# Results of the last three expert groups summed by one-hot matrices in PSUM, the row gathers of the others issued two groups earlier

## The chip, the core and the metric

The kernel runs on one core of one Trainium2 chip. The metric is the device time of one execution in microseconds (us). Engines: PE (matrix products), PEld (its weight loads), DVE (vector), ACT (scalar functions), POOL (general purpose, it also issues the indirect transfers on the software queue q0) and SP (issues the weight loads on the hardware queue q1). Tiles in SBUF have 128 partitions; products add up in eight PSUM banks of 128x512 f32, four called `pj` and four called `sc`.

## The reference

One block of a diffusion backbone over 512 latent tokens of width 1024 with 256 context tokens: two bidirectional recurrent mixers, then a mixture of 32 experts with two experts for a token, and a final norm. What concerns the change is the end:

```python
h_lat = h_lat + g1 * merge_branches(...)
h_lat = h_lat + g2 * hier_moe(modulate(rmsnorm(h_lat, norm_ffn), sh2, sc2), ...)
return rmsnorm(h_lat, norm_final)
# in hier_moe, for each expert e and the rows xb that go to it:
hid = silu(xb @ w_gate[e]) * (xb @ w_up[e])
y = hid @ w_down[e]
# each token gets the sum of its two rows y, each times its routing weight
```

## The kernel before

The experts' rows are packed into 18 groups of 128 slots, numbered 0 to 17 (`NG` is 18, `GROUPS` lists them): most groups hold two experts with 64 slots each, four hold one. Four experts are fixed to the first two groups, the others are put in by their count of tokens, the fullest first, so the last groups are the emptiest.

**The weights** of all experts are read once, 192 loads of 512 KB on SP (`feed`, L1122 and L1125), into a ring of 34 tiles called `raw` (`raw_tile`), in the order in which the products need them. A load waits for its tile to be free and for an earlier load to have landed.

**A group** g goes through `tokens` (its rows, gathered on POOL into `xg`, are transposed), `gate_up` (products L1156 into a `pj` bank, Silu on ACT, product on DVE: `hid`), `hidden` (transposes L1169, ACT copies `hT`, L1171) and `down` in two halves k of 16 products (L1180) into two `pj` banks. At the end of `down` DVE multiplies by the channel gate (`y`, L1189) and POOL scatters the rows to the table `ys_d` in DRAM, by token and choice (L1198). The loop interleaves: `gate_up(g)`, `down(g-1, 0)`, `hidden(g)`, `down(g-1, 1)`. For the last group (17) the rows are not scattered: `y` is multiplied by the slot's routing weight (L1194), split into two fp32r parts `yl` (ACT L1195, DVE L1196), and one-hot matrices `lsT` (made in `last_rows`, one 128x128 block for each of the four output tiles of 128 tokens) add them to the right tokens in PSUM (L1454).

**The end.** After `hidden(17)` `gather_results` issues eight gathers from `ys_d` (L986), two for each of the four output tiles i: one row for each choice of a token, 512 KB each, into free `raw` tiles `ya` and `yb`. The first waits for the scatter of group 16; a token whose expert is in the last group reads a row of zeros. `results` then sums: for tile 0 (`HD` is 1) DVE adds the weighted rows to the residual `hres` and then the PSUM banks; for tiles 1 to 3 PE first puts the residual into the bank by a product with the identity (L1452) and DVE adds the weighted rows to the bank (L1465, L1467). Then for each tile: ACT squares with a sum (L1468), a root (ACT L181, DVE L182 to L185), the product with the last norm's weights `nfin` and the root (tiles 0 and 1 on POOL L1471 and ACT L1472, tiles 2 and 3 on DVE L1474), and the output transfer on SP (L1475). An overflow block for experts with more rows than slots runs zero times with these inputs.

Instructions of an engine run in the order in which the scheduler put them. `issue_after(x)` keeps what it encloses behind instruction x in that order.

## Time and profile before

| | us |
|---|---|
| median of three runs | 1120.88 (1119.91 to 1122.23) |
| profiled execution | 1124.57 |
| its span in the profile | 1122.6 |
| PE busy | 1010.3 (90%) |
| DVE busy | 537.0 (48%) |
| ACT busy | 334.1 (30%) |
| POOL busy | 296.8 (26%) |

Times in the profile count from the start of the span. The experts' stage takes the time from some 850 us to the end. A share over the whole span says little about it; the stretches near the end and the DMA queues are to be read. DMA share is the mean busy share of the 16 DMA engines in a stretch.

### The profile page before, as it was taken

How to read it: one execution, taken by the hardware profiler on the slowest of the kernel's cores; microseconds unless marked ns; L12 is line 12 of the kernel's file. 1: busy time of each engine (PE TensorE's matmuls, PEld its weight loads, DVE VectorE, ACT ScalarE, POOL GpSimd, SP SyncE). 2: the span in 40 equal slices, each digit the busy share in tenths (PEclk: the TensorE clock that was granted, in tenths of full speed). 3: DMA queues.
4: the chain of work that ended last, by engine and by line, in shares of the span. 5: the costliest groups of instructions: out<-in, count | busy, mean ns of one | idle time of the engine just before them, and what ended most of it. 6: DMA issues, size and time to landing. Idle time of an engine off the chain costs nothing.

```text
span 1122.6 us, 17057 instructions
## 1 busy us (share of the span) xinstructions
PE 1010.3 (90%) x6574; PEld 825.9 (74%) x6574; DVE 537.0 (48%) x954; ACT 334.1 (30%) x580; POOL 296.8 (26%) x353
## 2 busy tenths in 40 slices
PE   3999899999899989999999999999837999999981
PEld 1679788799898978998977888889835665655430
DVE  4545677866788453554553341444461212212126
ACT  4237354554443213122323232332431101111003
POOL 1013235443536241415141100020431111110023
PEclk9999899999999999999999999999968999999996
DMA  9860213336224303341543161249159999999964
GB/s 303 210 207 20 57 38 95 94 95 207 57 76 114 95 19 94 111 134 38 151 136 108 40 177 65 86 158 379 53 194 385 409 405 399 393 391 401 403 260 181
DMA packets 111101, 203.19 MB, mean 181 GB/s; under 512 B 13147, under 2 KB 74925, under 8 KB 111018
## 3 DMA queue, kind: packets, MB, share of 16 engines
q1 hardware_dynamic: 98968, 180.53, 47.2%
q0 software_dynamic: 6320, 12.58, 3.1%
q10 hardware_dynamic: 5730, 8.98, 2.3%
q8 instruction: 52, 0.85, 0.3%
q14 instruction: 31, 0.25, 0.1%
HBM read 194.73 MB, written 17.31 MB: 189 GB/s over the span
## 4 chain that ended last, share of the span: by engine, by line
PE 29%; issue 19%; DVE 4%; POOL 3%; DMA 3%; ACT 0%; POOLq 0%; ACTq 0%; DVEq 0%
PE pj L341 16%; PE pj L332 9%; DMA raw<-ys_d,rowI 1%; POOL ys_d L1198 1%; POOL xg L986 1%; DMA xg<-xf_d,tokG 1%; DVE qs L594 1%; DVE oh L887 1%; PE sc L864 1%; DVE wl L1248 0%; PE sc L755 0%; PE sc L728 0%; DMA ys_d<-y,rowG 0%; DMA wada<-in_w_ada 0%; PE sc L555 0%
## 5 line engine op out<-in xcount | busy, mean ns | idle before, releaser
L332 PE MATMUL pj<-wh,xh 128*128 128x256 f32 x800 | 229.1, 286 | 3.6 <-ACT wh L1243 2.3
L332 PE MATMUL pj<-wl,xh 128*128 128x256 f32 x800 | 227.2, 285 | 0.3 <-DVE wl L1248 0.3
L332 PE MATMUL pj<-wh,xl 128*128 128x256 f32 x800 | 227.0, 284 | 0.0
L1248 DVE TENSOR_TENSOR wl<-raw,wh 128x1024 fp32r<-128x1024 f32 x88 | 118.5, 1354 | 93.0 <-ACT wh L1243 49.0
L332 PEld LDWEIGHTS pj<-wh,xh 128*128 128x128 f32 x800 | 153.8, 192 | 4.7 <-ACT wh L1243 2.5
L332 PEld LDWEIGHTS pj<-wh,xl 128*128 128x128 f32 x800 | 152.9, 191 | 0.6
L332 PEld LDWEIGHTS pj<-wl,xh 128*128 128x128 f32 x800 | 152.4, 191 | 0.7 <-DVE wl L1248 0.5
L1156 PE MATMUL pj<-raw,xt 128*64 128x256 f32 (+1 forms) x1024 | 135.0, 382 | 7.8 <-DMA raw<-in_w_expert_up 4.8
L1243 ACT CAST wh<-raw 128x1024 fp32r<-128x1024 f32 x88 | 91.4, 1048 | 168.7 <-PE pj L332 43.9
L1156 PEld LDWEIGHTS pj<-raw,xt 128*64 128x64 f32 (+1 forms) x1024 | 88.7, 143 | 53.4 <-DMA raw<-in_w_expert_up 8.1
L341 PE MATMUL pj<-xh,wh 128*128 128x512 f32 (+1 forms) x216 | 82.9, 388 | 3.3 <-ACT wh L1243 3.2
L341 PE MATMUL pj<-xl,wh 128*128 128x512 f32 (+1 forms) x216 | 82.8, 385 | 0.0
L341 PE MATMUL pj<-xh,wl 128*128 128x512 f32 (+1 forms) x216 | 82.5, 382 | 0.0
L341 PE MATMUL pj<-oT,wh 128*128 128x512 f32 x256 | 81.8, 399 | 0.8 <-ACT oT L760 0.5
L1180 PE MATMUL pj<-raw,hT 128*64 128x512 f32 (+1 forms) x256 | 75.8, 602 | 0.0
L703 DVE SCALAR_TENSOR_TENSOR adaacc<-wada,scT,adaacc 128x1024 f32<-128x1024 f32 x28 | 39.1, 1396 | 41.1 <-DMA wada<-in_w_ada 41.1
L341 PEld LDWEIGHTS pj<-oT,wh 128*128 128x128 f32 x256 | 48.3, 191 | 12.6 <-ACT oT L760 1.0
L341 PE MATMUL pj<-oT,wl 128*128 128x512 f32 x128 | 50.1, 394 | 0.0
L341 PEld LDWEIGHTS pj<-xh,wh 128*128 128x128 f32 x216 | 40.7, 190 | 11.0 <-ACT wh L1243 3.2
L1198 POOL DMA_INDIRECT ys_d<-y,rowG x17 | 16.9, 996 | 119.2 <-DVE y L1189 118.6
L423 POOL TENSOR_TENSOR th<-th,g 128x512 f32<-128x512 f32 x16 | 24.9, 1581 | 87.8 <-ACT th L422 87.8
L1189 DVE TENSOR_TENSOR y<-pj,adab 128x512 f32<-128x512 f32 x34 | 22.8, 689 | 51.5 <-PE pj L1180 51.5
(396 smaller groups left out, 1734.2 us busy)
## 6 DMA issues: line engine op xcount, KB each, us to landing
raw<-in_w_in SPq DMA_DIRECT2D x64, 512.0 KB
raw<-in_w_expert_up SPq DMA_DIRECT2D x64, 512.0 KB
raw<-in_w_expert_gate SPq DMA_DIRECT2D x64, 512.0 KB
raw<-in_w_expert_down SPq DMA_DIRECT2D x64, 512.0 KB
wada<-in_w_ada SPq DMA_DIRECT2D x32, 512.0 KB
wada<-in_w_ada SPq DMA_DIRECT2D x32, 256.0 KB
ys_d<-zero ACTq DMA_DIRECT2D x8, 512.0 KB
raw<-in_w_branch_gla SPq DMA_DIRECT2D x8, 512.0 KB
```

The costliest lines, as they stand in the source:

```text
L332: nc.tensor.matmul(out, x, (wh, wl)[wi][:, k], start=(start and first and k == 0 and n == 0), stop=(a == 1 and k == 3 and n == 2), skip_gr ...
L341: nc.tensor.matmul(out, (wh, wl)[wi][:, k, 128 * f:128 * (f + 1)], (th, tl)[xi][kk], start=(start and first and k == 0 and n == 0), stop=( ...
L423: nc.gpsimd.tensor_mul(th, th, g)
L594: nc.vector.tensor_mul(e, qT, qdec[:, None, o + 128 * h:o + 128 * (h + 1)].to_broadcast([128, 4, 128]))
L703: nc.vector.scalar_tensor_tensor(a, w, s, a, op0=OP.mult, op1=OP.add)
L864: nc.tensor.matmul(pl, hT[:, kk], wr[:, kk], start=(kk == 0), stop=(kk == NK - 1))
L1156: nc.tensor.matmul(p[r, u], st["x"][:, 4 * a + k, r], WT["gu", g, a, u, e][:, k], start=(a == 0 and u == 0 and k == 0), stop=(a == 1 and k ...
L1180: nc.tensor.matmul(st["p"][n2][r], st["h"][:, k, r], WT["d", g, k, 0, e][:, 512 * n2:512 * (n2 + 1)], start=(k == 0), stop=(k == 1))
L1189: nc.vector.tensor_mul(y[:, cs], st["p"][n2], ada_b[3][:, cs])
L1198: d = nc.gpsimd.indirect_dma_start(out=ys_d, out_offset=IOff(ap=rowG[:, g:g + 1], axis=0), in_=y, in_offset=None, bounds_check=ZROW - 1, o ...
L1243: nc.scalar.copy(parts[0], raw)
L1248: return nc.vector.tensor_sub(l, raws.pop(n), h)
```

## The change

`LAST` = 3 groups (15, 16, 17) now take the way that group 17 alone took: no scatter, but the slot's weight, a split into two fp32r parts (`tail`) and one-hot matrices (`LS["T"]`, three of them, made in `last_rows` in a loop over j). `gather_results` moves from behind `hidden(17)` to behind `gate_up(16)`: the gathers then wait for the scatter of group 14, and tokens of the last three groups read zeros. The new `early_sums` weights and adds the gathered rows to the residual ahead of the end: tiles 0 and 1 (`HD` = 2) on DVE, tiles 2 and 3 by scaled copies on ACT and adds on POOL. In `results` PE puts these sums into the banks of tiles 2 and 3 instead of the residual, and their squares and last norm read the banks directly. A root on ACT is issued before the end so that its table is loaded then.

```diff
-HD = 1
+HD = 2
+LAST = 3
...
 in down(g, k), after k == 1:
-            if g < NG - 1:
+        if g >= NG - LAST:
+            y = ring("y", g, 3, lambda: w4("y"))
+            h, l = (w4("tail", F32R) for _ in range(2))
+            tails.append((h, l))
+            w = LS["w"][:, g - NG + LAST:g - NG + LAST + 1]
+            for n2 in range(2):
+                cs = slice(512 * n2, 512 * (n2 + 1))
+                nc.vector.scalar_tensor_tensor(y[:, cs], st["p"][n2], w, ada_b[3][:, cs], op0=OP.mult, op1=OP.mult)
+                nc.scalar.copy(h[:, cs], y[:, cs])
+                last["part"] = nc.vector.tensor_sub(l[:, cs], y[:, cs], h[:, cs])
...
+    def early_sums(Y, r=range(4)):
+        for i in r:
+            ya, yb = Y[i]
+            if i >= HD:
+                for k, y in enumerate(Y[i]):
+                    nc.scalar.activation(y, y, AF.Copy, scale=wk[:, i, k:k + 1])
+                    nc.gpsimd.tensor_add(ya, y, hres[i] if k == 0 else ya)
+                continue
+            nc.vector.scalar_tensor_tensor(ya, ya, wk[:, i, 0:1], hres[i], op0=OP.mult, op1=OP.add)
+            nc.vector.scalar_tensor_tensor(ya, yb, wk[:, i, 1:2], ya, op0=OP.mult, op1=OP.add)
...
 in results(Y):
-                    nc.tensor.matmul(P[i, n], ident, hres[i][:, cs], start=True, stop=False)
+                    nc.tensor.matmul(P[i, n], ident, Y[i][0][:, cs], start=True, stop=False)
+            for j in range(LAST):
+                add(i, j)
...
+                s2 = small(1, "fs2")
+                for n, cs in enumerate(halves2):
+                    nc.scalar.activation(yb[:, cs], P[i, n], AF.Square, scale=1.0 / 32.0, accum_out=(s1, s2)[n])
...
 in the loop over g, after gate_up(g):
+            if g == NG - LAST + 1:
+                nfin = raw_tile(free)
+                nc.sync.dma_start(nfin, bass.AP(tensor=io["norm_final"].tensor, offset=io["norm_final"].offset,
+                                                ap=[[0, 128], [1, D]]))
+                Y = gather_results(lambda n: raw_tile(len(TL) + n))
...
         if g == NG - 1:
-            Y = gather_results(lambda n: raw_tile(free + 1 + n))
+            with tc.issue_after(last["hid"].ins), tc.issue_after(last["hT"].ins):
+                early_sums(Y, (0, 2, 3))
+            with tc.issue_after(last["part"].ins):
+                early_sums(Y, (1,))
+            with tc.issue_after(last["hT"].ins):
+                nc.scalar.activation(LS["r"], eps, AF.Sqrt)
```

**POOL, from the last gathers of tokens on.** `ys_d<-y` is a scatter, `raw<-ys_d` a gather of results. Before:

```order
L986 DMA xg<-xf_d,tokG 128x1024 x2
L1198 DMA ys_d<-y,rowG 1025x1024 x7
L986 DMA raw<-ys_d,rowI 128x1024 x8
L1471 TENSOR_TENSOR raw<-raw 128x1024 x2
L1075 TENSOR_LOAD extra
```

After:

```order
L987 DMA xg<-xf_d,tokG 128x1024 x2
L1203 DMA ys_d<-y,rowG 1025x1024 x5
L987 DMA raw<-ys_d,rowI 128x1024 x8
L1457 TENSOR_TENSOR raw<-raw,hres 128x1024
L1457 TENSOR_TENSOR raw<-raw 128x1024
L1457 TENSOR_TENSOR raw<-raw,hres 128x1024
L1457 TENSOR_TENSOR raw<-raw 128x1024
L1493 TENSOR_TENSOR raw<-raw 128x1024 x2
```

The gathers stand behind five scatters instead of seven, and four adds of the early sums stand between them and the products with `nfin`.

**ACT, from the last hT on** (the casts are the first fp32r parts of the last groups; `fs` are the sums of squares). Before:

```order
L1171 COPY hT<-sc 128x256
L1195 CAST yl<-y 128x512 x2
L1468 ACTIVATE raw,fs<-raw 128x1024
L181 ACT_TABLE_LOAD
L181 ACTIVATE fry<-fs,eps 128x1
```

After, with the tiles' numbers (`tail_9505` belongs to group 16, `tail_9536` to group 17):

```order
L1173 COPY hT_8014<-sc_9497 128x256
L1456 ACTIVATE raw_7782<-raw_7782,wk_191 128x1024
L1456 ACTIVATE raw_7784<-raw_7784,wk_191 128x1024
L1456 ACTIVATE raw_7786<-raw_7786,wk_191 128x1024
L1456 ACTIVATE raw_7788<-raw_7788,wk_191 128x1024
L1196 CAST tail_9505<-y_8047 128x512 x2
L1578 ACT_TABLE_LOAD
L1578 ACTIVATE wr_178<-eps_69 128x1
L1196 CAST tail_9536<-y_8201 128x512 x2
```

Four scaled copies of gathered rows (tiles 2 and 3) stand ahead of the casts of group 16, and the table load ahead of those of group 17.

**DVE, from the last hid on.** Before:

```order
L1162 TENSOR_TENSOR hid_7965<-hid_7965,pj_9369 128x256
L1189 TENSOR_TENSOR y_8047<-pj_9404,adab3_175 128x512
L1189 TENSOR_TENSOR y_8047<-pj_9405,adab3_175 128x512
L1194 SCALAR_TENSOR_TENSOR y_8201<-pj_9448,slotw_9241,adab3_175 128x512
L1194 SCALAR_TENSOR_TENSOR y_8201<-pj_9449,slotw_9241,adab3_175 128x512
L1196 TENSOR_TENSOR yl_9459<-y_8201,yl_9458 128x512
L1458 SCALAR_TENSOR_TENSOR raw_7786<-raw_7786,wk_191,hres_6774 128x1024
```

After:

```order
L1164 TENSOR_TENSOR hid_7965<-hid_7965,pj_9456 128x256
L1459 SCALAR_TENSOR_TENSOR raw_7665<-raw_7665,wk_191,hres_6774 128x1024
L1460 SCALAR_TENSOR_TENSOR raw_7665<-raw_7667,wk_191,raw_7665 128x1024
L1195 SCALAR_TENSOR_TENSOR y_8047<-pj_9491,wr_178,adab3_175 128x512
L1195 SCALAR_TENSOR_TENSOR y_8047<-pj_9492,wr_178,adab3_175 128x512
L1197 TENSOR_TENSOR tail_9506<-y_8047,tail_9505 128x512 x2
L1459 SCALAR_TENSOR_TENSOR raw_7768<-raw_7768,wk_191,hres_6776 128x1024
L1460 SCALAR_TENSOR_TENSOR raw_7768<-raw_7780,wk_191,raw_7768 128x1024
L1195 SCALAR_TENSOR_TENSOR y_8201<-pj_9526,wr_178,adab3_175 128x512
L1195 SCALAR_TENSOR_TENSOR y_8201<-pj_9527,wr_178,adab3_175 128x512
L1197 TENSOR_TENSOR tail_9537<-y_8201,tail_9536 128x512 x2
```

The sums of tile 0 come ahead of y of group 16, those of tile 1 ahead of y of group 17, and group 16 now has its two tail differences (L1197) there.

## Rows read from the trace of the kernel before

**Rows 1.** Busy time by stretch: columns named in the first row

```profile
core 0: us, PE busy (x) PEld busy (x) DVE busy (x) ACT busy (x) POOL busy (x), PEclk, DMA share, GB/s
1060.00:1070.00 10.00, 8.89 (x52) 4.14 (x50) 1.71 (x3) 0.76 (x2) 0.97 (x1) 1.00 1.02 404
1070.00:1080.00 10.00, 8.71 (x56) 4.10 (x52) 0.42 (x1) 0.38 (x1) 0.00 (x0) 1.00 1.01 397
1080.00:1085.00 5.00, 5.00 (x19) 2.20 (x18) 1.29 (x2) 0.37 (x1) 0.97 (x1) 1.00 0.27 111
400.00:404.00 4.00, 2.42 (x13) 1.51 (x11) 3.86 (x3) 0.00 (x0) 4.00 (x4) 1.00 0.00 0
404.00:408.00 4.00, 4.00 (x11) 3.20 (x12) 0.61 (x2) 0.00 (x0) 0.99 (x1) 0.57 0.00 0
```

**Rows 2.** Instructions in order of time, 1040 to 1124: start, us, engine, line [idle]

```profile
1051.86 0.97 POOL L1198 DMA_INDIRECT ys_d<-y,rowG  x1 [12.37 <-DVE y L1189]
...
1075.30 1.73 PE L1156 MATMUL pj<-raw,xt 128*64 128x256 f32 x13 [0.67 <-DMA raw<-in_w_expert_up]
...
1080.23 0.37 ACT L1171 COPY hT<-sc 128x256 f32<-128x256 f32 x1 [2.57 <-PE sc L1169]
...
1086.65 1.95 PE L1180 MATMUL pj<-raw,hT 128*64 128x512 f32 x8
...
1088.35 1.03 POOL L986 DMA_INDIRECT raw<-ys_d,rowI  x1 [3.73 <-issue]
1088.66 1.41 DVE L1194 SCALAR_TENSOR_TENSOR y<-pj,slotw,adab 128x512 f32<-128x512 f32 x2 [5.29 <-PE pj L1180]
...
1096.32 1.32 PE L1454 MATMUL pj<-yl,lsT 128*128 128x512 f32 x5
...
1109.80 1.06 ACT L1468 ACTIVATE raw<-raw 128x1024 f32<-128x1024 f32 x1
...
1112.52 1.28 DVE L1474 SCALAR_TENSOR_TENSOR raw<-raw,fry 128x1024 f32<-128x1024 f32 x1
```

**Rows 3.** DMA queues, 900 to 980: all, then the software queue

```profile
DMA packets 9852, 32.01 MB, mean 400 GB/s; under 512 B 2054, under 2 KB 2054, under 8 KB 9845
...
q0 software_dynamic: 2016, 3.41, 11.3%
```

**Rows 4.** The same, 980 to 1060; last row: scatters, us to landing

```profile
DMA packets 9518, 31.78 MB, mean 397 GB/s; under 512 B 1776, under 2 KB 1776, under 8 KB 9511
...
q0 software_dynamic: 1152, 1.24, 4.4%
...
ys_d<-y,rowG POOLq DMA_INDIRECT x6, 7.4
```

**Rows 5.** Chain of work that ended last: start, us, what

```profile
1083.64 3.65 DMA ys_d<-y,rowG
```

**Rows 6.** DMA queues, 1085 to 1123: packets, MB, share of 16 engines

```profile
q0 software_dynamic: 1296, 4.26, 31.9%
```

**Rows 7.** DMA queues of the page, whole span

```profile
q0 software_dynamic: 6320, 12.58, 3.1%
```

**Rows 8.** Groups by line, 1076 to 1123: busy us, mean ns, idle before

```profile
L1472 ACT ACTIVATE raw<-raw,fry 128x1024 f32<-128x1024 f32 x2 | 2.3, 1148 | 1.8 <-DVE fry L183 1.3 <-DVE fry L185 0.4
L1196 DVE TENSOR_TENSOR yl<-y,yl 128x512 fp32r<-128x512 f32 x2 | 1.4, 688 | 0.0
...
L1463 DVE TENSOR_TENSOR raw<-raw,sc 128x512 f32<-128x512 f32 x2 | 1.3, 680 | 0.0
```

**Rows 9.** Groups by line, POOL, whole span

```profile
L865 POOL TENSOR_TENSOR xf<-hres,adab 128x1024 f32<-128x1024 f32 x4 | 9.4, 2361 | 27.7 <-DVE hss L847 25.6 <-issue 2.2
```

**Rows 10.** Instructions in order of time, DVE beside POOL's product

```profile
1099.87 1.28 DVE L1467 SCALAR_TENSOR_TENSOR raw<-raw,wk 128x1024 f32<-128x1024 f32 x1
...
1100.44 6.21 POOL L1471 TENSOR_TENSOR raw<-raw 128x1024 f32<-128x1024 f32 x2 [1.55 <-ACT raw L1468]
...
1102.63 1.82 DVE L1467 SCALAR_TENSOR_TENSOR raw<-raw,wk 128x1024 f32<-128x1024 f32 x1
...
1104.37 2.30 DVE L184 SCALAR_TENSOR_TENSOR fra<-fry,frv 128x1 f32<-128x1 f32 x1
...
1107.51 0.21 DVE L184 SCALAR_TENSOR_TENSOR fra<-fry,frv 128x1 f32<-128x1 f32 x1
```

More of the change, by code (lines that the diff above doesn't have):

```diff
@@ L1161, in gate_up @@
         nc.scalar.activation(hid, p[:, 0], AF.Silu)
-        nc.vector.tensor_mul(hid, hid, p[:, 1])
+        last["hid"] = nc.vector.tensor_mul(hid, hid, p[:, 1])
         st["hid"] = hid
@@ L1170, in hidden @@
         h = m1k("hT", g).rearrange("p (k t) -> p k t", t=128)
-        nc.scalar.copy(h, p)
+        last["hT"] = nc.scalar.copy(h, p)
         st["h"] = h
@@ L1440, in gather_results, with add @@
         return y
+    def early_sums(Y, r=range(4)):
[8 more added lines that the diff above has]
+            nc.vector.scalar_tensor_tensor(ya, yb, wk[:, i, 1:2], ya, op0=OP.mult, op1=OP.add)
     def results(Y):
         P = {}
+        halves2 = [slice(512 * n, 512 * (n + 1)) for n in range(2)]
+        def add(i, j):
+            for n, cs in enumerate(halves2):
+                for m, x in enumerate(tails[j]):
+                    nc.tensor.matmul(P[i, n], LS["T"][j][:, i], x[:, cs], start=(i < HD and j == m == 0),
+                                     stop=(j == LAST - 1 and m == 1))
         for i in range(4):
[L1447 to L1449 removed]
+            for n, cs in enumerate(halves2):
                 P[i, n] = sc() if i < 2 else pj()
                 if i >= HD:
[L1452 to L1454 removed]
+                    nc.tensor.matmul(P[i, n], ident, Y[i][0][:, cs], start=True, stop=False)
+            for j in range(LAST):
+                add(i, j)
         for i, (ya, yb) in enumerate(Y):
@@ L1471, in results @@
                 nc.gpsimd.tensor_mul(yb, ya, nfin)
-                nc.scalar.activation(ya, yb, AF.Copy, scale=rs)
+                nc.scalar.activation(yb, yb, AF.Copy, scale=rs)
             else:
-                nc.vector.scalar_tensor_tensor(ya, ya, rs, nfin, op0=OP.mult, op1=OP.mult)
-            nc.sync.dma_start(io["out"][0, 128 * i:128 * (i + 1)], ya)
+                for n, cs in enumerate(halves2):
+                    nc.vector.scalar_tensor_tensor(yb[:, cs], P[i, n] if i >= HD else ya[:, cs], rs, nfin[:, cs],
+                                                   op0=OP.mult, op1=OP.mult)
+            nc.sync.dma_start(io["out"][0, 128 * i:128 * (i + 1)], yb)
     ada = late_ada()
```

84 lines of the change are left out of this document (35 added, 49 removed).

## The prediction

> **What bounds the kernel now.** I read three views in this order: the busy time by stretch near the end, the DMA queues of the same stage, and the instructions in order of time from the last products on.
>
> The stretches [rows 1] show that until 1080 us the 16 DMA engines are the limit: their share is 1.01 to 1.02 at 397 to 404 GB/s, while PE is busy 8.7 to 8.9 of 10 us. PE catches up with the stream: the last gate/up products start only when their weights land, after 0.67 us of waiting [rows 2]. After 1080 the stream is over (share 0.27). Two stretches of 80 us earlier in the same stage carry 3.41 and 1.24 MB on the software queue q0, and the total is 400 and 397 GB/s [rows 3, 4]: what the gathers and scatters move is taken from the weights, it does not come on top.
>
> From there the end is a chain [rows 2]. H, the copy of hT of the last group, ends at 1080.60. The last down product ends at 1088.60, 8.0 us after H. The last scatter lands 3.65 us after 1083.64 [rows 5], so the eight gathers start only at 1088.35. The last output tile is normed by 1113.80, which is H + 33.2, and 8.8 us of output transfer and program end follow to the span's 1122.6. The profiled execution took 1124.57 us, the median of the three runs is 1120.88; I work out a difference against the span and add it to the median.
>
> **The change part by part.**
>
> *The gathers move ahead of the weights' end.* They now wait for the scatter of group 14, issued at 1051.86 [rows 2], which lands some 7.4 us later in the full stream [rows 4], so at about 1060 instead of 1088. POOL issues nothing for the experts after that, so nobody on POOL queues behind them. But their bytes fall into the stretch where the DMA engines have no room. In the kernel before, q0 moved 4.26 MB after 1085 and kept all engines busy for 31.9% of 38 us, 12.1 us [rows 6]; at the 401 GB/s of the stage 4.26 MB are 10.6 us. Bounds: 0, if the engines found room, to 12.1. I take 10.6, the nearer stage. Against that one of the two dropped scatters (groups 15 and 16) lay in the stream: all gathers and scatters of tokens are 12.58 - 4.26 = 8.3 MB [rows 6, 7], in 35 transfers, so 0.24 MB or 0.6 us for one; these groups are the small ones, I take 0.3. Whether the weights of the last gate/up feel all of it depends on how the engines share. A scatter of the stage lands after 7.4 us [rows 4] against 3.65 in quiet [rows 5], so it is not put behind everything that is queued, and I take half and half: the 4.26 MB are through by 1060 + 21 = 1081, before the last gate/up weights, and H moves by **+10.3 us**.
>
> The rows cannot show the arbitration itself. The Trainium skill ("DMA: Bandwidth & Descriptors", Queues, rings and completion order) states that an engine goes round its queues packet by packet, which is the half and half of the sum; with the weights first the sum would be the second rival's. The same page (Specifications) gives a fabric ceiling of 435 GB/s; if the mix could reach it, 34 GB/s for 21 us would hide 0.7 MB and the term would be an estimated 1.8 us smaller, but the stage shows 400 at a share above 1, so the row stands.
>
> *One-hot matrices for three groups instead of one* (last_rows): 16 more small products, 8 more transposes and as many DVE comparisons, written among the products of group 15, some 30 us before H. PE has 1.1 to 1.3 us of slack in 10 [rows 1] and gets 10 more by the term above, so they cost nothing; without that cover they would cost a few us once.
>
> *From H to the last output.* ACT now runs four scaled copies of the gathered rows right after hT, 1.15 us each [rows 8], to H + 4.7, ahead of the casts of group 16; POOL adds each to the residual, four times 2.36 us [rows 9], from H + 1.2 on. DVE meanwhile has the two tail differences of group 16 (0.69 each [rows 8]), the sums of tile 1 (two of 1.28) and then the last y (1.41 [rows 2]). What happens when POOL and DVE both read two SBUF operands is in [rows 10]: a 1.28 us sum beside POOL's product takes 1.82, and a 128x1 step of 0.21 takes 2.30 and ends at 1106.67, when POOL's second product ends (1106.65); the two waited for each other in turn, one instruction each, and POOL's took 3.1 instead of 2.36. The first rows stretch the sum only a little, the last rows fully; I take the full alternation, since the tiny step lost all of the product's time. Then: adds 1 and 2 end at H + 5.9; the first difference ends at 6.6, add 3 at 9.0, the second difference at 9.7, add 4 at 12.0, DVE's tile-1 sums at 14.6, y at 16.0, its cast and differences at 17.4. PE's last down product stands behind the products of group 16, which need the second difference: 9.7 + 0.9 + 1.95 = 12.5, hidden under y's wait. The products of group 17 then run: 4 for the first two tiles, 12 for tile 2, two of the residual and 12 for tile 3, at 0.26 us each [rows 2] and about 0.5 for the fp32 two, so tile 2 is summed at 20.8 and tile 3 at 24.5. On ACT the order is square 0, root, square 1, scale 0, root, squares of tile 2, scale 1, root, squares of tile 3: DVE's adds (0.68 each [rows 8]) give tile 0 at 19.0, square 20.2, POOL's product 22.6, scale 0 at 24.1, tile 2's halves 26.1, scale 1 at 27.2, tile 3's halves from 27.5. The last tile needed 4.0 us from its square to the end before (1109.80 to 1113.80 [rows 2]); with a split square it is 4.7, so the last norm ends at H + 32.2. Before it was H + 33.2: **-1.0 us**. Without the alternation the same chain ends at H + 26.9, **-6.3 us**; these are the two ends. The early table load and the second tile with HD = 2 are inside these chains.
>
> The Trainium skill ("SBUF — State Buffer", Who interferes with whom) calls the port that DVE and GpSimd share an exclusive lock, held for a whole instruction by a GpSimd operation that reads SBUF and a DVE one with two SBUF inputs. By it the term is the -1.0; no row shows that such a step could run through a POOL add.
>
> Sum: +10.3 - 1.0 = +9.3 us, 1120.88 + 9.3 = **1130.2**.
>
> **The rivals.**
>
> 1. *No alternation* (the DVE steps fall between the adds): +10.3 - 6.3 = +4.0, 1124.9. For it: 0.7 us steps fit gaps while ACT feeds POOL. Against: ACT is ahead of POOL, so POOL has no gaps, and the 2.30 us step [rows 10].
> 2. *Weights first*: the gathers get little until the weights are in. H moves little, but rows 4 to 7 of Y then land near 1092 to 1094, ACT waits for them in front of the casts of group 16, PE's last down products and y stand behind; last norm some 6 us later than before, 1124.7 to 1126.7. This is also the case that the change does not do what it says: the sums run behind the products, not beside.
> 3. *Room in the DMA engines*, the other side: gathers move at 1060 to 1081 without delaying a weight, the delay is 0, and the tail gives 1.0 to 6.3 us: 1114.6 to 1119.9. Faster is decided where the delay is under 4 us with no alternation. Against: share 1.02 and the nearly equal totals of [rows 3, 4]; for: the one with more on q0 is 3 GB/s the higher.
> 4. *PE's clock*: at half rate of the weights PE waits some 3 us between bursts of 2 us. After a stretch with 2.42 busy of 4 us the granted clock was 0.57 in the next one (1.2 GHz would be 0.50) [rows 1]. If it is low at the last two down products (1.95 us each), up to 3.9 us more: 1134.
>
> **How the numbers follow.** Forecast 0.50 at 1130.2; rival 1 0.17; rival 2 0.13; rival 3 0.11; rival 4 0.09. Within 0.2% means 2.2 us, about what a measurement tells from no change, so 1118.6 to 1123.1. Faster: most of rival 3 and a shorter chain than worked out, 0.11. Same: the rest of rival 3 and the low end of rivals 1 and 2, 0.10. Slower: 0.79. Range: low 1121 leaves out rival 3; high is the 12.1 us bound with part of rival 4, 1120.88 + 12.1 - 1.3 + 3 = 1135.
>
> **What would show it.** In the trace after: gathers issued near 1060; q0 and q1 sharing about 400 GB/s from 1060 to 1081; PE waiting 2 to 4 us for gate and up weights in the last two groups instead of 0.6; the weights' end near 1091 and the copy of hT near 1091. If that copy still ends near 1081 to 1083 while the gathers have landed, the main term is wrong. For the tail: POOL adds of 3 us or more and a DVE difference or tile-1 sum of over 2 us; last norm 30 to 33 us after hT. If all DVE steps keep 0.7 and 1.3 us, rival 1 holds.

## The result and the profile after

The changed kernel takes 1137.75 us (median of four runs, 1133.25 to 1139.2) against 1120.54 us for the kernel before (four runs, 1119.91 to 1122.23): a ratio of 1.0144 with an interval of 1.0114 to 1.0175. Slower was right; the time lies above the range of the prediction (1121 to 1135). In a second comparison on another chip it was 1138.81 against 1128.14, a ratio of 1.0098 (1.0059 to 1.0136). The profiled execution took 1133.25 us, its span is 1131.4.

**Where to count from.** Raw times of two profiles can't be laid side by side: the stage ahead of the last groups ends several microseconds earlier or later in each execution, of one and the same kernel too. I count from W, the moment at which SP issues the first gate weights of the last group. This is the row of before, in order of time on SP (start, us, engine, line):

```profile
1055.09 1.62 SPq L1122 DMA_DIRECT2D raw<-in_w_expert_gate  x2
```

and of after, with the last expert weights that SP issues, eight loads of down weights (the columns are the same):

```profile
1050.98 1.62 SPq L1124 DMA_DIRECT2D raw<-in_w_expert_gate  x2
...
1061.23 9.84 SPq L1127 DMA_DIRECT2D raw<-in_w_expert_down  x8
```

W was 1055.09 and 1059.14 in two executions of before, 1050.98, 1056.64 and 1055.42 in three of after. From W to the end of the span the two of before need 67.5 and 69.0 us (mean 68.2), the three of after 80.4, 80.1 and 82.1 (mean 80.9). By this the change costs **12.6 us**; the forecast was 9.3. The timed differences, 17.2 and 10.7, lie around it. On the median of before 12.6 us would be 1133.1, inside the range; the 4.6 us beyond it lie ahead of W (in the second comparison this part is -1.9), and no run shows what sets W. So that the time lies above the range is owed to that part, and that 12.6 is near 9.3 is in part luck, since its parts are others:

| us after W | before | after |
|---|---|---|
| scatter of group 14 issued | -3.2 | +10.9 |
| first gather of results issued | +33.3 | +19.4 |
| H, end of the last copy of hT | +25.5 | +29.7 |
| y of group 17 begins | +33.6 | +53.0 |
| last norm ends | +58.7 | +71.7 |
| span ends | +67.5 | +80.4 |

H comes 4.1 us later, and from H to the last norm it takes 42.1 us instead of 33.2, 8.9 more. The forecast had 10.3 and -1.0.

**Why H is late.** Busy time of the engines in three stretches of after (columns as in [rows 1]), the middle one being that in which the products for the one-hot matrices are strung through those of group 15:

```profile
1030.00:1037.00 7.00, 5.93 (x37) 3.58 (x36) 4.81 (x20) 0.00 (x0) 1.03 (x1) 1.00 1.02 403
1037.00:1051.00 14.00, 13.83 (x57) 7.78 (x58) 3.71 (x16) 0.58 (x1) 0.00 (x0) 0.53 1.02 401
1051.00:1060.00 9.00, 9.00 (x57) 4.54 (x59) 1.02 (x2) 1.34 (x3) 0.00 (x0) 0.98 1.03 411
```

The granted clock falls to 0.53 for 14 us (0.50 is the lower level, 1.2 GHz) while PE is busy 13.83 of 14. PE's own rows (start, us, line, what, how many):

```profile
1028.24 0.95 PE L1227 MATMUL sc<-wk,lsh 128*128 128x1 f32 x8
...
1041.80 1.87 PE L1227 MATMUL sc<-wk,lsh 128*128 128x1 f32 x8
1043.60 1.12 PE L1158 MATMUL pj<-raw,xt 128*64 128x256 f32 x4
```

Eight of the small products (128x1 out) took 0.95 us at full clock and 1.87 here, and four gate/up products took 1.12 us (0.65 in e9 below, at full clock). The ACT row of `hid` that needs the products of group 15 begins at +5.3 by W (1056.30) instead of -10.2 (1044.85), 15.5 us late; the scatter of group 14 is issued at +10.9 instead of -3.2, 14.1 us late; `hid` of groups 16 and 17 is 9.9 and 4.9 us late, and H 4.1.

**Where the rows are.** POOL, in order of time: the scatter of group 14, the first of the eight gathers, the first and the last of the four adds:

```profile
1061.86 0.97 POOL L1203 DMA_INDIRECT ys_d<-y,rowG  x1 [26.97 <-DVE y L1202]
1070.38 1.03 POOL L987 DMA_INDIRECT raw<-ys_d,rowI  x1 [7.55 <-DMA raw<-in_w_expert_down]
...
1089.06 2.34 POOL L1457 TENSOR_TENSOR raw<-raw,hres 128x1024 f32<-128x1024 f32 x1 [8.09 <-ACT raw L1456]
...
1096.22 2.68 POOL L1457 TENSOR_TENSOR raw<-raw 128x1024 f32<-128x1024 f32 x1
```

The gathers stand 14 us later by W than the forecast put them (1060 less 1055.09, so +5), when nearly all gate/up weights are in. So they take next to nothing from those; the share of the DMA engines stays at 1.03 up to 1085, and the rows of tiles 2 and 3, which ACT scales, land after H (those of tile 0 are there at 1078.84, when DVE sums them). ACT, in order of time: copy of hT, the scaled copies of the rows, the casts of group 16 and those of group 17:

```profile
1080.26 0.37 ACT L1173 COPY hT<-sc 128x256 f32<-128x256 f32 x1 [1.80 <-PE sc L1171]
1087.83 1.15 ACT L1456 ACTIVATE raw<-raw,wk 128x1024 f32<-128x1024 f32 x1 [7.20 <-DMA raw<-ys_d,rowI]
1089.72 3.65 ACT L1456 ACTIVATE raw<-raw,wk 128x1024 f32<-128x1024 f32 x3 [0.74 <-DMA raw<-ys_d,rowI]
1093.28 1.12 ACT L1196 CAST tail<-y 128x512 fp32r<-128x512 f32 x2
...
1104.85 1.24 ACT L1196 CAST tail<-y 128x512 fp32r<-128x512 f32 x2 [8.94 <-issue]
```

Behind the copy of hT ACT has nothing before the scaled copies. It waits 7.2 us for the first row of tile 2 and then for the second, and the casts of group 16, whose y has been ready since 1085, stand behind them until 1093.28. What hangs on the casts, on DVE:

```profile
1093.91 5.53 DVE L1197 TENSOR_TENSOR tail<-y,tail 128x512 fp32r<-128x512 f32 x2 [9.00 <-ACT tail L1196]
...
1104.02 1.41 DVE L1195 SCALAR_TENSOR_TENSOR y<-pj,wr,adab 128x512 f32<-128x512 f32 x2 [2.06 <-PE pj L1182]
...
1121.29 1.41 DVE L1497 SCALAR_TENSOR_TENSOR raw<-pj,fry,raw 128x512 f32<-128x512 f32 x2
```

and on PE:

```profile
1093.93 0.79 PE L1470 MATMUL sc<-tail,lsT 128*128 128x512 f32 x1 [7.97 <-ACT tail L1196]
...
1101.50 2.44 PE L1182 MATMUL pj<-raw,hT 128*64 128x512 f32 x8
```

PE waited 7.97 us for the casts. Two differences that take 1.31 us alone (the row of group 17 at 1105.50) took 5.53 beside POOL's adds. PE's last down product, behind the products with these parts, ran at 1101.50 and y followed at 1104.02; the answering row of before is that of y in [rows 2], 1088.66. The last norm began at 1121.29 and ended at 1122.70. The stretches of after behind the stream (the last two rows have the lower clock):

```profile
1080.00:1085.00 5.00, 5.00 (x24) 2.17 (x24) 2.81 (x4) 0.37 (x1) 0.98 (x1) 1.00 1.03 413
1085.00:1090.00 5.00, 0.97 (x6) 0.08 (x2) 0.00 (x0) 1.43 (x2) 0.94 (x1) 0.89 0.47 190
1090.00:1095.00 5.00, 0.79 (x1) 0.29 (x1) 1.09 (x1) 4.77 (x6) 4.92 (x3) 0.50 0.02 9
1095.00:1100.00 5.00, 1.72 (x3) 1.00 (x4) 5.00 (x3) 0.91 (x2) 3.82 (x2) 0.50 0.00 0
```

The first of them is W + 29 to 34, and the same stretch of before (1084.1 to 1089.1) has a DMA share of 0.07 instead of 1.03. Then PE is busy for 3.5 of 15 us.

### The profile page after: what moved, and what is told of

Its sections match the earlier page's. It is cut to its first block, busy times and chain, and to the rows that moved or that the text cites. A ratio compares the mean times of both kernels' runs of the same rounds, so it can differ in the third digit from the quotient of the medians.

```text
span 1131.4 us, 17244 instructions
## 1 busy us (share of the span) xinstructions
PE 1024.5 (91%) x6642; PEld 837.3 (74%) x6642; DVE 546.6 (48%) x988; ACT 342.0 (30%) x595; POOL 303.4 (27%) x355
## 5 line engine op out<-in xcount | busy, mean ns | idle before, releaser
L1158 PE MATMUL pj<-raw,xt 128*64 128x256 f32 (+1 forms) x1024 | 138.2, 391 | 2.1 <-DMA raw<-in_w_expert_up 2.1
L1182 PE MATMUL pj<-raw,hT 128*64 128x512 f32 (+1 forms) x256 | 71.6, 606 | 0.0
L704 DVE SCALAR_TENSOR_TENSOR adaacc<-wada,scT,adaacc 128x1024 f32<-128x1024 f32 x28 | 39.5, 1409 | 42.3 <-DMA wada<-in_w_ada 42.3
L342 PEld LDWEIGHTS pj<-xh,wh 128*128 128x128 f32 x216 | 40.9, 190 | 10.9 <-ACT wh L1251 3.2
L342 PEld LDWEIGHTS pj<-xl,wh 128*128 128x128 f32 x216 | 41.1, 190 | 8.1 <-DVE xl L316 0.4
L342 PEld LDWEIGHTS pj<-xh,wl 128*128 128x128 f32 x216 | 41.1, 190 | 7.9 <-DVE wl L1256 0.5
## 6 DMA issues: line engine op xcount, KB each, us to landing
raw<-in_w_expert_up SPq DMA_DIRECT2D x64, 512.0 KB, 10.7
```

What stands on the lines that cost most here:

```text
L342: nc.tensor.matmul(out, (wh, wl)[wi][:, k, 128 * f:128 * (f + 1)], (th, tl)[xi][kk], start=(start and first and k == 0 and n == 0), stop=( ...
L704: nc.vector.scalar_tensor_tensor(a, w, s, a, op0=OP.mult, op1=OP.add)
L1158: nc.tensor.matmul(p[r, u], st["x"][:, 4 * a + k, r], WT["gu", g, a, u, e][:, k], start=(a == 0 and u == 0 and k == 0), stop=(a == 1 and k ...
L1182: nc.tensor.matmul(st["p"][n2][r], st["h"][:, k, r], WT["d", g, k, 0, e][:, 512 * n2:512 * (n2 + 1)], start=(k == 0), stop=(k == 1))
```

## The experiments

The theory after the first profile: (a) the early gathers do share the stream half and half, but in after they come too late to fall on H; (b) they come late because the one-hot work slows PE; (c) the rows then stop ACT in front of the casts. The main rival was the prediction's own sum: the stream term alone, whatever PE does. All times below are from W; ratios are against the kernel before on the same chip.

**The change again**, untouched, profiled once (e1), then profiled and timed (e5):

> The changed kernel once more, for a second trace. Clock theory: the 24 small products and 12 transposes of the one-hot matrices, written among group 15's products, bring the granted clock to 0.50 (in the first trace from 1037 to 1051 us), PE falls some 11 us behind, the scatter of group 14 and with it the gathers come some 10 us later than the weights allow, and the rows land at 1089. Then this trace shows 0.50 there again, and a run that is 4 to 6 us longer than the first has either a longer stretch at 0.50 or a second one nearer to the end. Stream theory (the forecast): the copy of hT of the last group is late because the gathers hold back the last gate and up weights; then PE waits on weights in the last two groups. 1133 to 1139 us by both.

> The changed kernel timed on this chip. Counted from W, the issue of the last group's first gate weights, the kernel before ends at W + 67.5 us and the changed one at W + 80.4 and W + 80.1 (two traces), so the change itself is worth 12.7 us; what the first comparison showed beyond that (17.2) would be where W fell by chance. Then the ratio here is 1.0113, some 12 to 13 us. If the change also moves W, it is 1.0144 again, 16 us or more.

Measured: 1138.45 us in the first, with the scatter of group 14 at +12.2, H at +34.4 and the end at +80.1; in the second the ratio 1.0098 told above, the scatter at +10.9, H at +29.7, the end at +82.1. The late scatter and the late end are there each time. The interval of 1.0098 holds the 1.0113 that was expected if W fell late by chance, and not the 1.0144 of the other reading. In the first, H was 4.7 us later than in the others, by a stop of ACT (last section), and the end was not: H does not set it, the copies of the rows do (they end at +42.4, +42.4 and +42.3 in the three).

**One matrix made, copied for the two other groups** (e2):

```diff
-        for j in range(LAST):
+        for j in (LAST - 1,):
...
+        for j in range(LAST - 1):
+            nc.scalar.copy(LS["T"][j], LS["T"][LAST - 1])
+            nc.vector.tensor_copy(LS["w"][:, j:j + 1], LS["w"][:, LAST - 1:LAST])
```

> Only group 17's one-hot matrix is worked out, as in the kernel before; those of groups 15 and 16 are copies of it, so 16 small products and 8 transposes are left out (the output then lacks the right rows of these two groups), and all else is as in the changed kernel. Clock theory: the granted clock stays 1.00 from 1020 to 1060 us, the scatter of group 14 is issued near 1048, the gathers near 1056, they now meet the last gate and up weights, so the copy of hT moves some 10 us (as the forecast had it) and the tail behind it takes 32 us instead of 42: 1130 us, and 1126 if the tail has no alternation. If the small products are not the cause: 1137 as the changed kernel.

Measured: ratio 1.0068 (1.0046 to 1.0090), end at +77.2. The output lacks the right rows of groups 15 and 16; the work on them behind their matrices is the same. The scatter is issued at -3.2 as before, the first gather at +4.6, and the clock is 1.00 from 1020 to 1070, in the stretch with the small products too:

```profile
1030.00:1040.00 10.00, 8.96 (x52) 4.68 (x53) 2.73 (x9) 0.76 (x2) 0.00 (x0) 1.00 1.01 402
```

Now the stream term falls where the prediction put it: PE waits for the last up weights.

```profile
1088.92 1.73 PE L1158 MATMUL pj<-raw,xt 128*64 128x256 f32 x13 [1.36 <-DMA raw<-in_w_expert_up]
```

DMA queues from 1068 to 1075 (packets, MB, share of 16 engines):

```profile
q1 hardware_dynamic: 381, 1.41, 51.9%
q0 software_dynamic: 365, 1.34, 49.2%
```

and SP's last eight loads:

```profile
1071.22 18.10 SPq L1127 DMA_DIRECT2D raw<-in_w_expert_down  x8
```

Each queue has half of the engines, with nearly as many packets as the other (381 and 365); issuing eight loads takes SP 18.10 us, where they took 9.84 in after. H is at +35.7, so it moved by 10.2 us, and from H to the last norm it takes 32.8; the prediction said 10.3 and 32.2. The steps between agree too: POOL's second and fourth add end 5.9 and 11.5 us after H (5.9 and 12.0 in the prediction), DVE's sums of tile 1 at 13.9 (14.6), y at 15.5 (16.0). Packet by packet is what the Trainium skill ("DMA: Bandwidth & Descriptors", Queues, rings and completion order) states; these rows agree.

**The one-hot work earlier**, at `g == 9`, so among the products of group 10 (e3):

```diff
-        if g == NG - 4:
+        if g == 9:
```

> All three one-hot matrices are worked out five groups earlier, among group 10's products instead of group 15's; nothing else moves. Clock theory: the stretch at 0.50 moves with them to some 80 to 90 us earlier, PE is level with the weights again before group 15, the rest as with one matrix: 1130 us. If the work itself costs PE the time wherever it stands, or the loss is in the tail alone: 1137.

Measured: 1.0073 (1.0044 to 1.0102), end at +79.8: the expectation fails. The stretches of this kernel (columns as above):

```profile
960.00:1000.00 40.00, 38.83 (x200) 23.04 (x198) 13.31 (x46) 2.39 (x6) 4.05 (x4) 0.74 1.03 405
...
1020.00:1060.00 40.00, 39.92 (x292) 22.86 (x290) 8.30 (x14) 4.03 (x9) 3.92 (x4) 1.00 1.01 397
```

The low clock came along (0.74 in the mean of 40 us), and PE did not catch up: it is busy 39.92 of 40 us from 1020 on, at full clock. By W, `hid` of group 10 is 20.5 us late and the scatter of group 14, at +9.0, still 12.2: in these groups there is little slack to catch up in, since PE of before is busy 94.61 of the 100 us from 960 to 1060.

**Is it the count of small products, or the four slots?** The kernel before writes its comparisons into eight slots, the change into four (`m % 4`), so that DVE must wait for PE before it writes the next four. First the kernel before with its one-hot work done three times (e9; `again` overwrites the same result):

```diff
+        for again in range(3):
+            pw = sc((128, 1))
...
```

> The kernel before, with its one group's one-hot matrix worked out three times over in the same place, so that only PE's 16 added small products and 8 added transposes and DVE's comparisons are new; gathers, sums and order are those of before. Small-products theory: group 15's products take some 14 us longer on PE (in the changed kernel the scatter of group 14 stood at W + 10.9 instead of W - 3.2, W being the issue of the last group's first gate weights), part of it is made good while PE has weights in stock, the copy of hT of the last group comes at W + 29 to 30 instead of W + 25.5, and the end at W + 70 to 72 instead of W + 67.5: 3 to 5 us slower than before. My own prediction's step (these products cost nothing): W + 67.5, no change.

Measured: 0.9984 (0.9959 to 1.0010), end at +68.3 (before 67.5 and 69.0). Its stretch with the small products:

```profile
1029.00:1043.00 14.00, 14.00 (x100) 9.65 (x100) 8.02 (x32) 2.13 (x4) 0.98 (x1) 1.00 1.01 395
```

The clock stays at 1.00, and H is at +25.6 (25.5 in before). But the scatter of group 14 is at +1.4 instead of -3.2 (W is 1052.38 here):

```profile
1053.73 0.98 POOL L1198 DMA_INDIRECT ys_d<-y,rowG  x1 [17.21 <-DVE y L1189]
```

So the count alone costs the end of this kernel nothing that can be told, and delays that scatter by 4.6 us. In before no gather waits for this scatter; in the change they all do. Then the change with eight slots (e12):

```diff
-        hr, hk = tb[:, 4:8], tb[:, 4:8].bitcast(F32)
+        hr, hk = tb, tb.bitcast(F32)
...
-                    nc.vector.tensor_scalar(hr[:, m % 4], iot, 1.0, lsm[:, m:m + 1], op0=OP.add, op1=OP.is_equal)
-                    nc.tensor.matmul(pw, hk[:, m % 4], wk[:, i, k:k + 1], start=(m == 0), stop=(m == 7))
+                    nc.vector.tensor_scalar(hr[:, m], iot, 1.0, lsm[:, m:m + 1], op0=OP.add, op1=OP.is_equal)
+                    nc.tensor.matmul(pw, hk[:, m], wk[:, i, k:k + 1], start=(m == 0), stop=(m == 7))
```

> The changed kernel with eight slots instead of four for the comparisons from which the one-hot matrices are made (the other half of the same tile is still free then), as the kernel before had them; the number of products, transposes and comparisons is the same. Hand-over theory: with four slots DVE must wait for PE's products before it can write the next comparisons and PE for DVE, so the 24 products and 12 transposes are drawn out through all of group 15's products, and in that stretch the granted clock fell to 0.50; with eight they stand close together, as in the kernel before with three times its work, where the clock stayed 1.00 and the scatter of group 14 came at W + 1.4. Then the clock stays 1.00 here until the last products, the scatter of group 14 is issued at W + 0 to 2 (W + 10.9 in the changed kernel), the gathers start near W + 9, meet the last gate, up and down weights, the copy of hT comes at W + 28 to 33, the rows are in at W + 34 to 37, and the end is W + 74 to 77 instead of W + 80.2. If the amount of small products is the cause, nothing moves: W + 80.

Measured: 1.0028 (1.0007 to 1.0049), end at +75.9. Its stretches:

```profile
1043.00:1050.00 7.00, 7.00 (x33) 4.09 (x33) 1.47 (x8) 0.58 (x1) 0.00 (x0) 0.54 1.03 404
1050.00:1057.00 7.00, 7.00 (x60) 4.52 (x59) 0.68 (x2) 0.97 (x2) 0.00 (x0) 0.97 1.02 408
```

The slots are worth 5.0 us of the 12.6 (80.9 to 75.9, one execution against three), and the scatter of group 14 comes at +4.2 instead of +10.9: 7.4 us late, where the count alone made 4.6 and four slots make 14.1. The end is in the expected +74 to +77; the scatter (+0 to +2) and the clock (1.00) are not as expected: the clock still fell for 7 us, half as long as with four slots. So the hand-over through four slots is shown to be one cause; what makes the clock fall when it does is not.

**Two groups instead of three** (e4):

```diff
-LAST = 3
+LAST = 2
```

> Two groups instead of three go by one-hot matrices, so the gathers wait for the scatter of group 15 and stand behind the last gate and up products: they are issued when nearly all weights are in. Stream theory: the last gate and up weights are all in before the gathers start, the copy of hT moves by 0 to 2 us, the rows land near 1090, the tail gives some us back: 1117 to 1123. Clock theory: two thirds of the small products leave a shorter stretch at 0.50, PE is a few us late as well: 1121 to 1128.

Measured: 1.0072 (1.0044 to 1.0101), end at +79.7, far from the expected 1117 to 1123 us. H is back at +25.6, and nothing is won. ACT in order of time:

```profile
1077.57 0.37 ACT L1173 COPY hT<-sc 128x256 f32<-128x256 f32 x1 [2.57 <-PE sc L1171]
1090.38 1.15 ACT L1456 ACTIVATE raw<-raw,wk 128x1024 f32<-128x1024 f32 x1 [12.44 <-DMA raw<-ys_d,rowI]
...
1095.36 1.12 ACT L1196 CAST tail<-y 128x512 fp32r<-128x512 f32 x2
```

The gathers wait for the scatter of group 15 (+12.8) and go out at +20.6; ACT waits 12.44 us for the first row of tile 2, and the casts come at 1095.36, 43.0 us after W; in after 42.3. This bears (c) out: the casts behind the rows come as late with H in its old place as with H late.

**The early sums behind the last y**, with three groups (e6) and with two (e7, the same edit and `LAST = 2`):

```diff
-            with tc.issue_after(last["hid"].ins), tc.issue_after(last["hT"].ins):
-                early_sums(Y, (0, 2, 3))
-            with tc.issue_after(last["part"].ins):
-                early_sums(Y, (1,))
...
+    with tc.issue_after(last["part"].ins), tc.issue_after(last["cast"].ins):
+        early_sums(Y)
```

> As the changed kernel with three groups by one-hot matrices, but all early sums (ACT's copies, POOL's adds, DVE's sums of tiles 0 and 1) stand behind the last group's y and its differences instead of in front of the casts of group 16. Queue theory: ACT's copies, which wait for the gathered rows, hold up the casts of group 16, PE's last down product and the last y, and the 28 to 29 us from the last copy to the last norm are a chain in which only some 12 us need the rows. Then the last norm comes at W + 58 to 62 instead of W + 71, the program ends at W + 67 to 71, and the time is 0 to 4 us above before. If the rows' landing alone set the end, or the two engines' alternation at the port, little changes: W + 77 or more.

> The same order with two groups by one-hot matrices: the gathers start behind all weight loads (the copy of hT stood at W + 25.6 there, as before the change), the rows land by W + 39.5, y and its differences are done by W + 36. Then ACT's copies end at W + 44, POOL's adds at W + 49 to 51, the last norm at W + 56 to 59, the end at W + 65 to 68: 0 to 3 us below before. If only the weights' stream counted, it would end as the earlier run with two groups did, at W + 79.7.

Measured: 1.0065 (1.0036 to 1.0094), end at +75.3, and 1.0047 (1.0020 to 1.0074), end at +74.1. Both had been expected lower (+67 to +71 and +65 to +68). The order is worth 5.6 us in both (80.9 to 75.3, 79.7 to 74.1); that is ACT's copies together with POOL's adds and DVE's sums, which moved with them. The ratios on this chip put it at 3.7 us with three groups (1.0098 to 1.0065) and 2.8 with two (1.0072 on another chip to 1.0047). What is left shows on DVE (e6; L1459 and L1460 are the sums, two each, 1.28 us apiece alone):

```profile
1098.77 4.57 DVE L1459 SCALAR_TENSOR_TENSOR raw<-raw,wk,hres 128x1024 f32<-128x1024 f32 x2
1103.26 6.64 DVE L1460 SCALAR_TENSOR_TENSOR raw<-raw,wk 128x1024 f32<-128x1024 f32 x2
```

and on POOL beside it:

```profile
1102.33 3.20 POOL L1457 TENSOR_TENSOR raw<-raw 128x1024 f32<-128x1024 f32 x1
1105.49 3.32 POOL L1457 TENSOR_TENSOR raw<-raw,hres 128x1024 f32<-128x1024 f32 x1
```

Four sums take 11.2 us instead of 5.1, four adds 12.8 instead of 9.4 (2.36 each). That is the full alternation of [rows 10]: adds of 3.0 to 3.3 us, as the prediction worked out.

**No scaled copies and no adds** (e8): two groups; the early sums are dropped, and all four tiles are summed at the end as tiles 1 to 3 were before.

```diff
-HD = 2
-LAST = 3
+HD = 0
+LAST = 2
...
-                    nc.tensor.matmul(P[i, n], ident, Y[i][0][:, cs], start=True, stop=False)
+                    nc.tensor.matmul(P[i, n], ident, hres[i][:, cs], start=True, stop=False)
...
+                    nc.vector.scalar_tensor_tensor(ya[:, cs], ya[:, cs], wk[:, i, 0:1], P[i, n], op0=OP.mult, op1=OP.add)
+            if i >= HD:
+                nc.vector.scalar_tensor_tensor(ya, yb, wk[:, i, 1:2], ya, op0=OP.mult, op1=OP.add)
```

> Two groups by one-hot matrices and the gathers behind the last gate and up products, but no early sums at all: the sums are made as in the kernel before, by DVE from PSUM, with the residual of all four tiles put in PSUM by PE. DVE needs 2.6 us for a tile's sum. Rows land by W + 39.5, the last tile is summed at W + 43 to 46 and normed at W + 48 to 51, the end is W + 57 to 60: 7 to 10 us below before, 1117 to 1120. If the rows' landing is not what the sums wait for, the time is that of before.

Measured: 0.9964 (0.9935 to 0.9992), end at +67.1, 12.6 us less than e4 (+57 to +60 was expected). One row on DVE and the row on POOL that it meets, the product with `nfin`:

```profile
1101.75 3.07 DVE L1489 SCALAR_TENSOR_TENSOR raw<-raw,wk 128x1024 f32<-128x1024 f32 x1
```

```profile
1101.37 2.37 POOL L1493 TENSOR_TENSOR raw<-raw 128x1024 f32<-128x1024 f32 x1 [11.07 <-ACT raw L1490]
```

A sum of two SBUF tiles, 1.28 us alone, takes 3.07 beside one product of POOL; this happens twice (3.12 the second time).

**Eight slots, and the sums written in PSUM**, with two groups (e13), with one (e14, gathers back in their old place) and with three (e15). On the e8 way of summing:

```diff
+                    nc.vector.scalar_tensor_tensor(P[i, n], ya[:, cs], wk[:, i, 0:1], P[i, n], op0=OP.mult, op1=OP.add)
+                    nc.vector.scalar_tensor_tensor(ya[:, cs], yb[:, cs], wk[:, i, 1:2], P[i, n], op0=OP.mult, op1=OP.add)
```

> The version that was the best so far (two groups by one-hot matrices, gathers behind the last gate and up products, sums by DVE from PSUM, end at W + 67.1), with eight comparison slots, and with each tile's first sum written back to PSUM, so that no sum of DVE reads two operands from SBUF beside POOL's two norm products. Port theory: the two sums that took 3.07 and 3.12 us beside POOL's products (1.28 alone) take two times 0.74, some 3 us less on the chain; the scatter of group 15 comes 2 us earlier with the slots. Last norm at W + 52 to 55 instead of W + 58.0, end at W + 61 to 64, 4 to 7 us below before. If the order on DVE or PE's last products set the end: W + 66 to 67.

> The sums of the best version (residual in PSUM, both rows added by DVE with at most one operand from SBUF, eight slots) with one group by its one-hot matrix and the gathers at their old place behind the scatter of group 16. If the earlier gathers are what makes that version faster than before, this one ends at W + 66 to 69, within 2 us of before. If it is the sums, it ends at W + 62 to 65 and is 3 to 5 us below before: rows land at W + 46 to 49 and DVE then needs no more than 8 us to the last norm.

> The same sums with three groups by one-hot matrices and the gathers where the changed kernel has them: the change's own idea without its order on ACT, DVE and POOL. Stream theory: the copy of hT comes at W + 30 to 35, as in the run with eight slots (W + 31.0), because the gathers meet the last weights; rows are in by W + 38, PE's last products at W + 50, the last norm at W + 60 to 64, the end at W + 69 to 73: 2 to 5 us above before and slower than with two groups. If the order alone cost the time, it ends at W + 62 to 66, level with two groups or below.

Measured: two groups 0.9951 (0.9931 to 0.9971), end at +66.5; one group 0.9963 (0.9939 to 0.9987), end at +68.5; three groups 0.9986 (0.9961 to 1.0010), end at +71.6. The slots show here too: with two groups and four slots (e8) the clock is 0.54 from 1044 to 1051 and the scatter of group 14 at +3.5; with eight (e13) the clock is 1.00 from 1030 to 1065 and the scatter at -1.9. DVE in e13 (L1488 reads a PSUM bank in place of the second SBUF tile; L185 is a 128x1 step):

```profile
1103.98 0.75 DVE L1488 SCALAR_TENSOR_TENSOR raw<-raw,wk,sc 128x512 f32<-128x512 f32 x1
1104.64 1.34 DVE L185 SCALAR_TENSOR_TENSOR fra<-fry,frv 128x1 f32<-128x1 f32 x1
```

and POOL:

```profile
1103.60 2.37 POOL L1492 TENSOR_TENSOR raw<-raw 128x1024 f32<-128x1024 f32 x1 [14.66 <-ACT raw L1489]
```

The sum beside POOL's product keeps its 0.75 us, while the step of 0.22 us with two SBUF inputs right behind it takes 1.34 and ends with the product. This is the lock that the Trainium skill ("SBUF — State Buffer", Who interferes with whom) describes for two SBUF inputs; the rows agree, and one PSUM input is outside of it. The two-group kernel was expected at +61 to +64 and is at +66.5, because PE now waits inside its last products (the other value that the expectation named, +66 to +67). On PE:

```profile
1085.24 1.94 PE L1182 MATMUL pj<-raw,hT 128*64 128x512 f32 x8
...
1093.09 3.59 PE L1182 MATMUL pj<-raw,hT 128*64 128x512 f32 x8
```

Eight products take 1.94 us, and 3.40 and 3.59 where their last down weights land among the gathers: q0 has 59.7% and q1 40.1% of the DMA engines from 1079 to 1095. The clock is not the reason here, it is 1.00 from 1085 to 1100. So e13 is ahead of both kernels, but how much of it comes from the early gathers is not settled: the one-group kernel, which gathers as late as before, has a ratio that overlaps, and by W the two are 2.0 us apart. With three groups the end is 3.1 us later than with one (71.6 less 68.5), inside the +69 to +73 expected; the expected ratio above before is not there, the two ratios overlap, and e15 has the low clock of the one-hot work again (0.66 from 1040 to 1050). So that early gathers cost something with three groups is not shown either.

**The rows by products on PE** (e10, two groups; e11, one group): a diagonal matrix of routing weights for each tile and choice, and the rows summed by fp32 products instead of by DVE.

```diff
+        LS["D"] = tb.bitcast(F32)
+        for m in range(8):
+            nc.vector.tensor_scalar(LS["D"][:, m], ident, wk[:, m // 2, m % 2:m % 2 + 1], None, op0=OP.mult)
...
+                    for k in range(2):
+                        nc.tensor.matmul(P[i, n], LS["D"][:, 2 * i + k], Y[i][k][:, cs], start=False, stop=(k == 1))
```

> Two groups by one-hot matrices, gathers behind the last gate and up products, and the sums made by PE alone: the gathered rows are multiplied into PSUM by diagonal matrices that hold their weights, so no engine scales or adds rows, POOL does nothing behind the gathers, ACT squares from PSUM and DVE norms from PSUM. Queue-and-port theory: what followed the landing of the rows was the order on ACT and DVE and the alternation of DVE and POOL (with early sums in front the end was W + 79.7, with late sums W + 74.1, with DVE sums W + 67.1). Without them the last products stand some 2 us behind the rows at W + 40 to 43, the last norm at W + 48 to 52, the end at W + 57 to 61, 6 to 10 us below before. If the landing of the rows and the weights' stream set the end, no more than 2 us are to be had against the version with DVE's sums.

> The same sums by PE with one group by its one-hot matrix and the gathers at their old place behind the scatter of group 16: it tells how much of the gain is the sums and how much the earlier gathers. Queue-and-port theory: rows land at W + 46 to 49 as before, the last norm comes some 7 us after that, at W + 53 to 56 instead of W + 58.7: 3 to 6 us below before, and 3 to 5 above the version with two groups.

Measured: 1.0031 (1.0004 to 1.0058), end at +72.4, and 0.9996 (0.9973 to 1.0019), end at +67.9. Both miss: +57 to +61 and 3 to 6 us below before were expected. In e10 PE becomes the bound:

```profile
1099.55 7.03 PE L1481 MATMUL sc<-raw,lsh 128*128 128x512 f32 x16
```

That row and its twin for the other two tiles are 14 us of products one behind the other, where DVE needs 11.8 for 16 sums of 0.74. With one group nothing is gained or lost that these runs could tell.

**Before against itself** (e16), for the error of the yardstick:

> The kernel before against itself, with a profile on the chip of the experiments: the yardstick. So far it rests on one trace from another chip (copy of hT at W + 25.5, gathers from W + 33.3, last norm at W + 58.7, end at W + 67.5). If the yardstick holds, the end is at W + 67 to 68.5 and the ratio 1.000 within 0.3%, and the versions at W + 66.5 to 68.5 differ from before by no more than their ratios say. If this kernel's end lies at W + 70 or later here, the distances of all versions from before are 2 to 4 us better than the single trace made them.

Measured: 0.9984 (0.9969 to 1.0000), end at +69.0. So a ratio within some 0.3% of 1 tells nothing here, and an end within some 2 us of another neither (three executions of after lie between 80.1 and 82.1).

## Why the prediction was wrong, point by point

**One-hot matrices "cost nothing"**: this step failed first. I read the number of instructions in the diff and not `m % 4`: DVE and PE hand four slots to and fro, the work is drawn out over all of `gate_up(15)`, and the granted clock is at the lower level for 14 us. The slack, too, was read in the wrong place: 1.1 to 1.3 us in 10 stand in [rows 1] for 1060 to 1080, while the work goes in 30 us before H, where before has this (columns as in [rows 1]):

```profile
1030.00:1040.00 10.00, 10.00 (x69) 5.96 (x69) 3.25 (x9) 1.02 (x3) 0.97 (x1) 1.00 1.00 395
1040.00:1050.00 10.00, 10.00 (x62) 5.20 (x59) 1.02 (x2) 1.34 (x3) 0.00 (x0) 1.00 1.03 398
```

PE has no idle time at all there. So even the count of products, which the prediction had right, delays the scatter of group 14 by 4.6 us (e9), "a few us once" as it says of the case without cover; with four slots it is 14.1. The cover that I named, 10 us of waiting for weights, can only come after the gathers, whose own scatter is behind the late products. The sum had no term for it, and took 1060 for the gathers as if the scatter did not move. The step is worth 3.7 us of the end (80.9 to 77.2 in e2, which is one execution; 5.0 with eight slots and all products). Without it (e2) the sum meets the profile: +10.2 and 32.8 against +10.3 and 32.2, an end 9.0 us later than before against 9.3.

**The stream term, +10.3**: right as a mechanism (e2: 51.9 and 49.2%), and it did not happen in after. The gathers went out at +19.4, H moved by 4.1 us, and for PE's lateness. "Gathers issued near 1060" was the sign I had asked for, W + 5; they are issued at 1070.38, W + 19.4.

**The tail, -1.0**: counted from H, with the rows taken as landed. In after those of tiles 2 and 3 land from +37 on, 7 us behind H, and the ACT order that I had written down myself (copies ahead of the casts of group 16) turns that into 42.1 us from H to the last norm. Only e6 and e7 give its price, 5.6 us by W. Where the rows are in time (e2), the same order takes 32.8 us. One count was wrong without effect: the products of group 17 for the first two tiles are 8 in the trace, not 4. The full alternation was right in kind (5.53 us for two differences; all of it in e6), and rival 1 is out; its size in after was smaller for POOL, whose adds took 2.34 to 2.68 us instead of 3.1, and larger for the two differences.

**The rivals.** What happened is the second half of rival 2: rows late, ACT waiting in front of the casts, the sums behind the products instead of beside. I had tied it to "weights first", which is not so, gave it 6 us and 0.13; the same wait came through late gathers and cost 12.6 with the slowed PE. Rival 3 (room in the DMA engines) is out by e2. Rival 4 was looked for in the last down products, where it cost 0.5 us (2.44 for 1.95; 1.7 in the two other executions, 3.69 and 3.66); the low clock that mattered was 50 us earlier, in a stretch in which PE was busy.

**The range** ended at the 12.1 us of the stream term with part of rival 4. No bound stood for the one-hot work; [rows 1] has a stretch at a clock of 0.57, and the small products at half the clock would have been one.

The parts of the 12.6 us that were changed one at a time: eight slots -5.0, sums behind y -5.6, each from single executions that differ by up to 2 us; both, with the sums as in e15, leave 3.4 of it (71.6 against 68.2). Why the clock falls, and what moved the 4.6 us ahead of W, stays open.

## What to carry to other kernels

Before small products are said to fit into an engine's slack, read its slack in the stretch in which they will stand, and not in a later one. Then count the buffers between the engine and the one that makes their operands, and look at the slot count of old code when it is looped. A transfer that is moved earlier starts when its own producer is done, so work out the producer's new time first, and put nothing that waits for the transfer in front of work that is ready on the same engine's queue. Where DVE and POOL run side by side, let DVE's second operand come from PSUM if it can.

## What the runs showed of the hardware

The granted clock fell to the lower level while PE was busy 13.83 of 14 us with small fp32 products between gate/up products, and for 7 us with eight slots; the same products in the kernel before, busy 14.00 of 14, left it at 1.00 (e9), and so did eight slots with two groups (e13). What tells the stretches apart for the chip stays open.

In two executions ACT stopped for some 4 us with its operand ready. ACT's row in e1 (its wait is put down to nothing on this core):

```profile
1089.19 0.38 ACT L1163 ACTIVATE hid<-pj 128x256 f32<-128x256 f32 x1 [8.87 <-remote]
```

and the queues from 1084 to 1090:

```profile
q0 software_dynamic: 580, 2.10, 88.6%
q1 hardware_dynamic: 84, 0.30, 12.4%
q8 instruction: 1, 0.02, 1.1%
```

One packet of instructions travels in a stretch in which the gathers hold 88.6% of the DMA engines; that ACT waits for its own instructions behind the gathers fits, but is only argued, and after has such a packet too, from 1080 to 1085, in a stretch in which ACT waits for rows. The same stop is in e3 (8.65 us of idle time before the row of `hid`), and in none of the other profiled executions.
